# A two-layer encoder on one core: two kinds of 64-row matrix products become 128-row products

## The chip, the cores and the metric

The kernel runs on one core of one Trainium2 chip. The metric is the device time of one execution in microseconds (us), the median over several runs. A TensorE product of a 128-row operand contracts over 128 partitions, that is over all rows of the array; a 64-row product contracts over 64 partitions and uses half the rows. "Rows" of an operand are partitions throughout, and "columns" is the length that streams through the array (256 or 512 here).

## The reference

The program computes two residual layers for x of 1024 steps by 1024 features: layer 0 is a bidirectional Hyena mixer (a gated long convolution by FFT), layer 1 a bidirectional Mamba-2 SSD mixer. The change touches layer 0 alone, in the network that makes the convolution's filters and in the first stage of the transforms:

```python
def hyena_filters(L, w1, b1, w2, b2, w3, b3, freq, w_out):
    ...
    h = jnp.sin(fr * (h @ w3.astype(jnp.float32) + b3))
    h = h @ w_out.astype(jnp.float32)
    ...
    h = h * jnp.exp(-t * jnp.concatenate([deltas, deltas]))
    return h[:, :D_INNER], h[:, D_INNER:]

def bidirectional_fftconv(u, h_fwd, h_bwd, skip):
    ...
    k_f = jnp.fft.rfft(kfull, n=n, axis=0)
    u_f = jnp.fft.rfft(uf32, n=n, axis=1)
    y = jnp.fft.irfft(u_f * k_f[None], n=n, axis=1)[:, :L]
    return y + uf32 * skip.astype(jnp.float32)
```

The hidden layer has 64 features, D_INNER is 2048, L is 1024.

## The kernel before

Matrix products run on float32r operands. Each float32 operand is split into a high part H of 12 significant bits and a low part L, and a product is H.H + H.L + L.H, summed in PSUM. A name that ends in h or l is such a part (`xh`, `xl`, `wh`, `wl`, `tah`, `tal`).

**Two parts on top of each other.** Where only 64 rows are contracted, the parts can share the 128 rows. The filter network's last hidden layer, `hs`, holds H in one half of the partitions and L in the other. A product of `hs` over all 128 rows with the output weights' high part `wfh`, stacked twice, gives H.H + L.H at once. What is missing, H.L, is a second product with the low part `wfl`, over the 64 rows that hold H. In `stage1` these are lines 375 and 376, twice per task, 512 columns each. The first stage of the forward transform does the same in `hyena_fft` from its later calls on: line 589 multiplies the input's stacked parts by `tau`, the table's high part stacked twice, and line 590 the input's high half by `tal`, the table's low part (64 rows, 256 columns), four such pairs per task. Earlier calls, before `tau` is loaded, use three 64-row products (line 592).

**Stages of layer 0.** From about 62 to 317 us the filters are made: for each of 4 blocks of 512 channels, 8 tasks `stage1` (lines 368 to 399: filter products, times a decay `dec` to `kr` on VectorE, split into `xh`, `xl`, three products with `tah`/`tal`, copy to `asb`, to DRAM as `ask`) and 16 tasks `stage2` (load `bs` from `ask`, split, products with `tbh`/`tbl`, copy, to DRAM as `kd`). After that, for 8 blocks of 256 channels: `hyena_mid` (tasks "m", which load `k` from `kd`), `hyena_fft` (tasks "a") and `hyena_back` (tasks "b", whose products with `tai` at lines 642 and 643 have 128 rows and 256 columns), in the order of the list `todo`. The projections of x (line 261, 3072 products of 128 rows and 512 columns) are laid between these tasks by `fill`, a fixed number of quarters per step, so that TensorE has work while a task's other engines run.

**Order.** A scheduler puts the program's instructions into one fixed order per engine when it is built, and each engine then takes its own in that order. Loads and stores are issued by SyncE (SP) in one order; the tables come over GpSimd (POOL). `TB = 12` says before which item of `todo` the table `tau` is fetched; a one-element copy on POOL makes that fetch wait for a product's result (`self.mark`).

**Memory.** `tah` lies in a pool at the right side that is closed when the filters are done. `tal` lies in the pool `h0` that lives as long as layer 0's mixer. The tables and tiles of the later tasks lie in the pool `h1`, opened when the filters are done.

Of the kernel before, what the change touches and what calls it, by code (L numbers as in the profile page):

```python
"""Hybrid encoder trunk, two layers on one core: a bidirectional Hyena layer, then a bidirectional
Mamba-2 SSD layer, each with its DeepNorm residual.

Matrix products run on float32r operands: each float32 operand is split into a high part of 12
significant bits and the rest (x = H + L), and a product is H.H + H.L + L.H in float32 PSUM.

Hyena's long convolution is evaluated at the 1024 points z_g = exp(-2 pi i (g + 1/4) / 1024). With
z^1024 = -i the products of a real signal and a two-sided real kernel wrap into the imaginary part,
so one complex transform of length 1024 gives the linear convolution of length 2048. The transform
is two stages (64 x 16) of matrix products, with t = 16 t1 + t2 and g = g1 + 64 g2.  # L10
"""
# [9 lines left out]
F32 = mybir.dt.float32  # L21
F32R = mybir.dt.float32r
AF = mybir.ActivationFunctionType
ALU = mybir.AluOpType
PSUM = bass.MemoryType.PSUM
DRAM = bass.MemoryType.DRAM

L = 1024
# [6 lines left out]
TA = 3  # L35
# [53 lines left out]
def _round12(a):  # L89
    """float64 -> float32 values with 12 significant bits, nearest even."""  # L90
    m, e = np.frexp(a)
    return np.ldexp(np.rint(m * 4096.0), e - 12).astype(np.float32)
# [40 lines left out]
def _constants():  # L133
# [4 lines left out]
    # both parts side by side, the high one first where n2 is even  # L138
# [34 lines left out]
class Pipe:  # L173
    """Tasks under way, each a generator that yields between its stages; a step moves each by a stage."""
# [15 lines left out]
class Build:  # L190
    def __init__(self, tc, a, p, pp, dp):
        """p, pp, dp: pools in SBUF (weights' tiles), PSUM and DRAM for the whole program."""
        self.tc, self.nc, self.a, self.p, self.pp, self.dp = tc, tc.nc, a, p, pp, dp
        self.ident = p.tile([128, 128], F32, name="ident")
        self.nc.sync.dma_start(out=self.ident, in_=a["ident"])
        self.ready = lambda k: True
        self.mhalf = p.tile([128, 1], F32, name="mhalf")
        self.nc.vector.memset(self.mhalf, -0.5)
# [7 lines left out]
    def weights(self, src, gain=None, pool=None, bufs=2, name="w"):  # L206
        """128 x 1024 (or 512) weights in two parts, times a gain per row if there is one."""
# [14 lines left out]
    def split(self, src, h, l):  # L222
        """h + l = src, both float32r."""
# [3 lines left out]
    def pair(self, pool):  # L227
        """The two parts' tiles of [128, 512] values."""
        return pool.tile([128, 512], F32R, name="xh", bufs=XB), pool.tile([128, 512], F32R, name="xl", bufs=XB)

    def load_pair(self, pool, src):
        """[128, 512] values from DRAM in two parts."""
# [12 lines left out]
    def load_r(self, pool, name, shape, src):  # L245
        """A float32r tile from float32 values that have 12 significant bits."""
# [4 lines left out]
    def projections(self, work, ahead, xh, xl):  # L251
        """Projections of x^T, each [128 channels, 1024] in PSUM for its function; a step per quarter of one."""
# [17 lines left out]
    def filter_mlp(self, pm, hs):  # L270
        """The filter network's last hidden layer at 16 n1 + n2 and at 1024 - (16 n1 + n2), in two parts on top of
        each other."""
# [45 lines left out]
    def filters(self, kd, sh, t):  # L318
        """The convolution kernels' transforms, to kd[block][re/im][64][16][256]; yields the tasks of each step."""
# [3 lines left out]
        def stage2(cb, j):  # L323
            # the last of the first stage's results go to DRAM two steps after their task's first
# [17 lines left out]
        with tc.tile_pool(name="k0", bufs=1) as p:  # L342
# [5 lines left out]
            with tc.tile_pool(name="k1", bufs=1) as p:  # L348

                def consts(cb):  # L350
                    cs = slice(512 * cb, 512 * cb + 512)
                    wfh = [p.tile([128, 512], F32R, name=f"wfh{q}", bufs=2) for q in range(2)]
                    wfl = p.tile([128, 512], F32R, name="wfl", bufs=2)
                    for q in range(2):
# [4 lines left out]
                        nc.scalar.copy(wfh[q], wr)  # L359
                        r = slice(64 * q, 64 * q + 64)  # L360
                        nc.vector.tensor_tensor(out=wfl[r], in0=wr[r], in1=wfh[q][r].bitcast(F32), op=ALU.subtract)
# [6 lines left out]
                def stage1(cb, m, k):  # L368
                    """The kernels at n2 = 2 m and 2 m + 1, and their transforms' first stage."""
                    wfh, wfl, delta, skip = k  # L370
                    ks = [p.tile([128, 512], F32, name=f"kr{i}", bufs=KRB) for i in range(2)]
                    for q in range(2):
                        ps = self.bank()
                        r, c = slice(64 * q, 64 * q + 64), slice(128 * m, 128 * m + 128)
                        nc.tensor.matmul(ps, hs[:, q, c], wfh[q], start=True, stop=False)
                        nc.tensor.matmul(ps, hs[r, q, c], wfl[r], start=False, stop=True)  # L376
# [35 lines left out]
    def hyena(self, yt, after):  # L412
        """Layer 0's mixer up to its output projection: from x^T (permuted time) to y^T in DRAM."""
# [4 lines left out]
        with tc.tile_pool(name="h0", bufs=1) as p, tc.tile_pool(name="hf", bufs=1, space=PSUM) as self.pf:  # L418
# [17 lines left out]
            for n, s in (("ta", [128, 16, 128]), ("tb", [128, 128]), ("tbi", [128, 128])):  # L436
                for q in "hl":
                    t[n + q] = (pa if n + q == "tah" else p).tile(s, F32R, name=n + q)
                    flat = t[n + q].rearrange("p a b -> p (a b)") if len(s) == 3 else t[n + q]
                    if n == "ta":  # L440
                        # not before x
# [5 lines left out]
            def u_work(b):  # L447
                """x1 * v for 256 channels."""
# [9 lines left out]
            def q_work(b):  # L458
                """x0 * silu(z) for 256 channels."""
# [14 lines left out]
            def fill(n):  # L474
                """Projections up to n quarters in all."""
# [23 lines left out]
            with tc.tile_pool(name="h1", bufs=1) as pf:  # L499
                tabs = [(i, n, pf.tile(s, F32R, name=n), d) for i, n, s, d in (  # L500
                    (TA, "tai", [128, 16, 128], "tai"), (TB, "tau", [128, 16, 128], "tauh"))]
# [17 lines left out]
                for i, item in enumerate(todo):  # L519
                    if tabs and i == tabs[0][0]:  # L520
                        # a table's load waits for the products under way
# [41 lines left out]
    def hyena_fft(self, sh, t, us, spill, pb2):  # L563
        """A quarter of the first stage of the transform of 256 channels, to DRAM."""
# [7 lines left out]
        both = "tau" in t  # L572
# [11 lines left out]
        for i in range(2):  # L584
            for hf in range(2):
                n2 = 4 * pb2 + 2 * i + hf
                r = slice(64 * hf, 64 * hf + 64)
                if both:
                    nc.tensor.matmul(pa[hf][:, i], t["tau"][:, n2], u[hf][:, i], start=True, stop=False)
                    nc.tensor.matmul(pa[hf][:, i], t["tal"][r, n2], u[hf][r, i], start=False, stop=True)  # L590
# [8 lines left out]
    def hyena_mid(self, sh, p, t, kd, b, spill, vspill, j):  # L599
        """The transform's second stage, its product with the filters', and the inverse's first, to DRAM."""  # L600
# [29 lines left out]
    def hyena_back(self, sh, p, t, yt, b, vspill, qs, gs, pb2):  # L630
        """A quarter of the inverse's second stage times qs, to yt in the order of time."""
# [44 lines left out]
    def ssd(self, h1t, wdt, yt, after):  # L676
        """Layer 1's mixer up to its output projection: from h1^T to the normed y^T in DRAM; the first steps of what
        comes after are taken beside its last chunks."""
        tc, nc, a = self.tc, self.nc, self.a
        with tc.tile_pool(name="s", bufs=1) as p, tc.tile_pool(name="sf", bufs=1, space=PSUM) as self.pf:  # L680
# [10 lines left out]
            # the exponents' factors: in each direction, rows of ones (2), of the columns' terms (16)  # L691
            # against rows of the sums (2), and of the heads' places (16); odd chunks in the lower half
# [9 lines left out]
            # whether y^T's rows k, k + 1 are in DRAM for the first blocks  # L702
# [6 lines left out]
            # B, C, B^T and x at each chunk  # L709
# [19 lines left out]
            def flow():  # L729
# [7 lines left out]
                def column(ps, w, k, halves):  # L737
                    """What one k adds to 128 channels."""
# [5 lines left out]
                # the first two go through the first half of the time, then through the second  # L744
# [33 lines left out]
            def fill(n):  # L778
                """The order's units up to n quarters in all."""
# [18 lines left out]
            with tc.tile_pool(name="sc", bufs=1) as self.ps:  # L798
# [9 lines left out]
                def places(g):  # L808
                    """The group's rows of the exponents' factors."""
# [13 lines left out]
                for n in range(4):  # L823
# [4 lines left out]
                    else:  # L828
                        # the projections' input has been read
# [26 lines left out]
    def ssd_dt(self, p, h1t, t, wdt):  # L856
        """dt, the chunks' running sums of dt * a in both directions, and what follows of them."""
# [6 lines left out]
        # the second half of the time lies below the first: 64 heads x 512 steps each  # L864
# [32 lines left out]
        def columns(src):  # L897
            """[128, 2, 4, 64]: the heads along each row of the chunks."""
# [48 lines left out]
        def spread(c):  # L947
            """The chunk's exp(running sums) to DRAM, its heads of a parity together."""
# [395 lines left out]
```

## Time before, and how to read the profile

| | |
|---|---|
| time, median of 3 runs | 2263.41 us (2261.83 to 2263.8) |
| profiled execution, first to last instruction (span) | 2258.7 us |
| median less the span | 4.7 us |
| TensorE (PE) busy in the span | 2161.1 us (96%) |
| weight loads (PEld), beside the products | 1676.8 us (74%) |
| VectorE (DVE) | 1596.6 us (71%) |
| ScalarE (ACT) | 1172.2 us (52%) |
| GpSimd (POOL) | 333.5 us (15%) |
| mean granted TensorE clock | 0.981 |

The profiled execution has no time of its own in the records beside its span; what lies around the span is taken as the 4.7 us by which the median is longer.

In the views, `L376` is line 376 of the kernel, `64*128 64x512` is a product whose stationary operand has 64 rows and 128 columns and whose moving operand has 64 rows and 512 columns. A product's record starts when its turn in the array's queue comes, and its modelled end overlaps the next one's start, since products are pipelined. So what a product costs its engine is read from one start to the next, not from the duration. PEclk is the granted clock: 1.00 is the higher of the two levels, 2.4 GHz, 0.50 the lower, 1.2 GHz.

### The profile page before, as it was taken

The page shows a single profiled execution, that of the slowest core. Times are in us where ns is not written, and L with a number is a line of the kernel's source. Part 1 is how long each engine was busy: PE and PEld are TensorE (multiplying, and loading weights), DVE is VectorE, ACT ScalarE, POOL GpSimd, SP SyncE. Part 2 cuts the span into 40 slices and gives each one's busy share as a digit, 9 for nine tenths or more (in the row PEclk, how much of TensorE's full clock was granted, in tenths as well). Part 3 has the DMA queues.
Part 4 walks back from the last instruction along what each step waited for, and adds up shares of the span by engine and source line. Part 5 has one row for each costly group of instructions (what it writes and reads, how often), then busy time and mean ns, then how long its engine had stood idle before and what let it go on. Part 6 is the DMA issues. An engine that isn't in the chain of part 4 may idle for free.

```text
span 2258.7 us, 28866 instructions
## 1 busy us (share of the span) xinstructions
PE 2161.1 (96%) x9930; PEld 1676.8 (74%) x9930; DVE 1596.6 (71%) x2269; ACT 1172.2 (52%) x1688; POOL 333.5 (15%) x390
## 2 busy tenths in 40 slices
PE   8999999999999999999999997999999998887897
PEld 5677677878787878778777776777777776565686
DVE  7888877676766768657866564764876877765665
ACT  4677775455655555446654343645455555333442
POOL 0000000000000000000000102333344445534000
PEclk9999999999999999999999998999999999888999
DMA  6266778565656556557686425434455455446863
GB/s 201 100 216 229 238 250 258 174 195 159 188 156 177 167 161 177 149 167 207 232 303 202 147 64 156 124 110 127 142 153 163 154 150 166 147 156 197 265 218 128
DMA packets 261423, 399.26 MB, mean 177 GB/s; under 512 B 31879, under 2 KB 158599, under 8 KB 260765
## 3 DMA queue, kind: packets, MB, share of 16 engines
q1 hardware_dynamic: 247677, 391.38, 55.6%
q0 software_dynamic: 13600, 6.04, 1.2%
q8 instruction: 79, 1.29, 0.2%
q14 instruction: 67, 0.55, 0.1%
HBM read 280.64 MB, written 116.65 MB: 176 GB/s over the span
## 4 chain that ended last, share of the span: by engine, by line
PE 80%; DMA 9%; DVE 6%; ACT 2%; issue 2%; POOL 1%; SPq 0%; POOLq 0%; DVEq 0%; ACTq 0%
PE pj L261 31%; PE pj L743 16%; PE pj L1193 5%; PE pk L1193 5%; PE f L241 3%; PE f L242 3%; PE f L243 3%; DMA wr<-l_w_out 3%; DMA bx<-bxd 2%; PE f L1024 2%; PE f L1085 1%; PE f L996 1%; PE f L590 1%; PE f L1059 1%; PE f L376 1%
## 5 line engine op out<-in xcount | busy, mean ns | idle before, releaser
L261 PE MATMUL pj<-xth,wh 128*128 128x512 f32 x1024 | 329.3, 400 | 1.8 <-ACT xth L224 1.8
L261 PE MATMUL pj<-xtl,wh 128*128 128x512 f32 x1024 | 328.5, 398 | 1.4 <-DVE xtl L225 1.4
L261 PE MATMUL pj<-xth,wl 128*128 128x512 f32 x1024 | 325.6, 395 | 0.0
L215 DVE TENSOR_TENSOR wl<-wr,wh 128x1024 fp32r<-128x1024 f32 x152 | 192.1, 1266 | 153.0 <-ACT wh L214 151.3
L214 ACT CAST wh<-wr 128x1024 fp32r<-128x1024 f32 x152 | 159.5, 1049 | 190.0 <-PE pj L261 60.7
L261 PEld LDWEIGHTS pj<-xtl,wh 128*128 128x128 f32 x1024 | 192.3, 189 | 48.7 <-issue 4.6
L261 PEld LDWEIGHTS pj<-xth,wl 128*128 128x128 f32 x1024 | 192.2, 188 | 46.7 <-issue 4.6
L261 PEld LDWEIGHTS pj<-xth,wh 128*128 128x128 f32 x1024 | 188.6, 189 | 45.1 <-issue 3.8
L743 PE MATMUL pj<-h1th,wh 128*128 128x512 f32 x640 | 217.3, 413 | 0.9 <-DVE cv L671 0.9
L743 PE MATMUL pj<-h1th,wl 128*128 128x512 f32 x640 | 207.0, 400 | 0.0
L743 PE MATMUL pj<-h1tl,wh 128*128 128x512 f32 x640 | 206.9, 401 | 0.0
L225 DVE TENSOR_TENSOR xl<-bs,xh 128x512 fp32r<-128x512 f32 x192 | 129.2, 686 | 60.3 <-ACT xh L224 59.2
L1241 POOL TENSOR_SCALAR rs<-mv 128x1 f32<-128x1 f32 x16 | 8.3, 518 | 1019.8 <-DMA wr<-l_w_out 740.3
L224 ACT CAST xh<-bs 128x512 fp32r<-128x512 f32 x192 | 117.5, 620 | 67.5 <-PE f L642 29.0
L743 PEld LDWEIGHTS pj<-h1th,wh 128*128 128x128 f32 x640 | 118.8, 192 | 40.5 <-issue 18.6
L743 PEld LDWEIGHTS pj<-h1tl,wh 128*128 128x128 f32 x640 | 122.2, 192 | 28.4 <-issue 2.7
L743 PEld LDWEIGHTS pj<-h1th,wl 128*128 128x128 f32 x640 | 122.5, 193 | 27.2 <-issue 1.4
L559 DVE SCALAR_TENSOR_TENSOR cv<-pj,cw,cv 128x960 f32<-128x960 f32 x192 | 139.2, 744 | 4.8 <-ACT cv L556 2.7
L671 DVE SCALAR_TENSOR_TENSOR cv<-pj,cw,cv 128x1023 f32<-128x1023 f32 (+1 forms) x96 | 122.5, 1276 | 6.2 <-ACT cv L668 5.7
L1193 PE MATMUL pj<-wh,yh 128*128 128x512 f32 x320 | 105.5, 411 | 16.9 <-ACT wh L217 9.3
L1193 PE MATMUL pj<-wl,yh 128*128 128x512 f32 x320 | 104.5, 406 | 2.5 <-DVE wl L218 2.0
L1193 PE MATMUL pj<-wh,yl 128*128 128x512 f32 x320 | 102.8, 403 | 0.0
(264 smaller groups left out, 4226.2 us busy)
## 6 DMA issues: line engine op xcount, KB each, us to landing
wr<-w SPq DMA_DIRECT2D x104, 512.0 KB
wr<-l_w_out SPq DMA_DIRECT2D x96, 512.0 KB
k<-kd SPq DMA_DIRECT2D x256, 128.0 KB
ask<-asb SPq DMA_DIRECT2D x64, 256.0 KB
bs<-ask SPq DMA_DIRECT2D x64, 256.0 KB
kd<-asb SPq DMA_DIRECT2D x64, 256.0 KB
as<-asb SPq DMA_DIRECT2D x64, 256.0 KB
bs<-as SPq DMA_DIRECT2D x64, 256.0 KB
```

What stands on the lines that cost most here:

```text
L214: nc.scalar.copy(wh, wr)
L215: nc.vector.tensor_tensor(out=wl, in0=wr, in1=wh.bitcast(F32), op=ALU.subtract)
L224: self.nc.scalar.copy(h, src)
L225: self.nc.vector.tensor_tensor(out=l, in0=src, in1=h.bitcast(F32), op=ALU.subtract)
L241: mm(out, ah, bh, start=start, stop=False)
L242: mm(out, ah, bl, start=False, stop=False)
L243: mm(out, al, bh, start=False, stop=stop)
L261: self.nc.tensor.matmul(ps[:, t], lhs[:, k], rhs[:, k, t], start=st, stop=sp)
L559: nc.vector.scalar_tensor_tensor(out=acc[:, o], in0=ps[:, i], scalar=cw[:, w:w + 1], in1=acc[:, o], op0=ALU.mult, op1=ALU.add)
L671: nc.vector.scalar_tensor_tensor(out=acc[:, o], in0=ps[:, i], scalar=cw[:, w:w + 1], in1=acc[:, o], op0=ALU.mult, op1=ALU.add)
L743: nc.tensor.matmul(ps[:, c], lhs[:, k], rhs[:, k, c], start=st, stop=sp)
L1193: nc.tensor.matmul(po[hf], lhs[:, t], rhs[:, c], start=s, stop=e)
```

## The change

The low parts get the same form as the high ones. `wfl` becomes two tiles of 128 rows (the output weights' low part stacked twice, one tile for each of the two halves q), and line 376 multiplies all 128 rows of `hs` with it. The transform's low table is loaded stacked twice as well (`taul`, a new 1 MB load; the array that it comes from is there before), and line 590 multiplies all 128 rows. The sum then holds L.L besides. `tal`, which only the filters and the earlier calls of `hyena_fft` now use, moves to the pool that is closed with `tah`.

```diff
-                    wfl = p.tile([128, 512], F32R, name="wfl", bufs=2)
+                    wfl = [p.tile([128, 512], F32R, name=f"wfl{q}", bufs=2) for q in range(2)]
...
-                        nc.scalar.copy(wfh[q], wr)
-                        r = slice(64 * q, 64 * q + 64)
-                        nc.vector.tensor_tensor(out=wfl[r], in0=wr[r], in1=wfh[q][r].bitcast(F32), op=ALU.subtract)
+                        self.split(wr, wfh[q], wfl[q])
...
-                        r, c = slice(64 * q, 64 * q + 64), slice(128 * m, 128 * m + 128)
+                        c = slice(128 * m, 128 * m + 128)
...
                         nc.tensor.matmul(ps, hs[:, q, c], wfh[q], start=True, stop=False)
-                        nc.tensor.matmul(ps, hs[r, q, c], wfl[r], start=False, stop=True)
+                        nc.tensor.matmul(ps, hs[:, q, c], wfl[q], start=False, stop=True)
...
-                    t[n + q] = (pa if n + q == "tah" else p).tile(s, F32R, name=n + q)
+                    t[n + q] = (pa if n == "ta" else p).tile(s, F32R, name=n + q)
...
-                    (TA, "tai", [128, 16, 128], "tai"), (TB, "tau", [128, 16, 128], "tauh"))]
+                    (TA, "tai", [128, 16, 128], "tai"), (TB, "tauh", [128, 16, 128], "tauh"), (TB, "taul", [128, 16, 128], "taul"))]
...
-                    if tabs and i == tabs[0][0]:
+                    while tabs and i == tabs[0][0]:
...
-        both = "tau" in t
+        both = "taul" in t
...
-                    nc.tensor.matmul(pa[hf][:, i], t["tau"][:, n2], u[hf][:, i], start=True, stop=False)
-                    nc.tensor.matmul(pa[hf][:, i], t["tal"][r, n2], u[hf][r, i], start=False, stop=True)
+                    nc.tensor.matmul(pa[hf][:, i], t["tauh"][:, n2], u[hf][:, i], start=True, stop=False)
+                    nc.tensor.matmul(pa[hf][:, i], t["taul"][:, n2], u[hf][:, i], start=False, stop=True)
```

Apart from names and a shift of lines by one, the engines' orders are the same in both programs but for three places. The first is none of order but of operands: TensorE's first filter products, at the start of the stage from 62 us on. Before:

```order
L375 MATMUL f<-wfh_292,hs 128x512
L376 MATMUL f<-wfl,hs 128x512
L375 MATMUL f<-wfh_291,hs 128x512
L376 MATMUL f<-wfl,hs 128x512 x2
L375 MATMUL f<-wfh_292,hs 128x512
L376 MATMUL f<-wfl,hs 128x512
```

With the change:

```order
L374 MATMUL f<-wfh_292,hs 128x512
L375 MATMUL f<-wfl_293,hs 128x512
L374 MATMUL f<-wfh_291,hs 128x512
L375 MATMUL f<-wfl_294,hs 128x512
L375 MATMUL f<-wfl_293,hs 128x512
L374 MATMUL f<-wfh_292,hs 128x512
L375 MATMUL f<-wfl_294,hs 128x512
```

The products stand as they stood; the two that read one tile `wfl` before (its two halves) read a tile each now. (The shape printed is the output's, so it does not tell the rows.)

The second place is POOL's fetch of the tables, from `tai` on. Before:

```order
L523 CAST tai<-asb 1x2
L524 DMA tai<-tai 128x2048
L523 CAST tau<-asb 1x2
L524 DMA tau<-tauh 128x2048
```

With the change:

```order
L522 CAST tai<-asb 1x2
L523 DMA tai<-tai 128x2048
L522 CAST tauh<-asb 1x2
L522 CAST taul<-asb 1x2
L523 DMA tauh<-tauh 128x2048
L523 DMA taul<-taul 128x2048
```

The second table's one-element copy and its load stand beside the first's.

The third place is SP's queue at the end of the filters, where the first load of `k` for `hyena_mid` stands among the last block's stores (`ask`, `kd`) and loads (`bs`). Before, with what each row waits for:

```order
L340 DMA kd<-asb 128x2x256 [waits DMAHW1_49,DVE_49]
L397 DMA ask<-asb 128x512 [waits DMAHW2_49,Activation_49]
L340 DMA kd<-asb 128x2x256 [waits DMAHW3_49,Activation_49]
L609 DMA k_3480<-kd 64x512 [waits DMAHW4_49]
L340 DMA kd<-asb 128x2x256 [waits DMAHW5_49,DVE_49]
L234 DMA bs<-ask 128x512 [waits DMAHW6_49,DMAHW2_49,DMAHW0_49]
```

With the change:

```order
L340 DMA kd<-asb 128x2x256 [waits DMAHW0_49,DVE_49]
L396 DMA ask<-asb 128x512 [waits DMAHW1_49,Activation_49]
L340 DMA kd<-asb 128x2x256 [waits DMAHW2_49,Activation_49]
L608 DMA k_3485<-kd 64x512 [waits DMASW5_49,DMASW4_49,DMAHW3_49,PE_49,Pool_49]
L608 DMA k_3485<-kd 64x512 [waits DMAHW4_49]
L340 DMA kd<-asb 128x2x256 [waits DMAHW5_49,DVE_49]
L234 DMA bs<-ask 128x512 [waits DMAHW7_49,DMAHW6_49,DMAHW1_49]
```

The first half of the first `k` stood five stores earlier before; now both halves stand behind the last store of `ask`, and the tile's memory is that in which `tah` and `tal` lay (it waits for their loads, for TensorE and for POOL). Some dozens of rows of the engines around this place stand a few positions earlier or later for it. Beyond that only one split of weights at the start of layer 1 changes places with two others.

## Rows read from the trace of the kernel before

**Rows 1.** The page's head: the span and the number of instructions.

```profile
span 2258.7 us, 28866 instructions
```

**Rows 2.** Busy time by stretch; columns: engines' busy us (instructions), PEclk, DMA share.

```profile
60.00:310.00 250.00, 249.93 (x1016) 175.37 (x1015) 216.76 (x318) 183.35 (x310) 0.00 (x0) 1.00 0.61 202
310.00:490.00 180.00, 178.24 (x796) 144.52 (x796) 134.54 (x196) 100.87 (x156) 1.41 (x4) 1.00 0.72 221
490.00:1005.00 515.00, 514.84 (x2332) 409.79 (x2331) 348.78 (x501) 275.87 (x426) 0.00 (x0) 1.00 0.57 167
...
2000.00:2100.00 100.00, 74.27 (x305) 54.78 (x304) 54.08 (x77) 31.41 (x44) 33.89 (x34) 0.86 0.65 196
```

**Rows 3.** TensorE's waits, whole span: us in total, times, longest.

```profile
PE f L241 <- ACT xh L224: 1.8, 4, 0.8
```

**Rows 4.** Timeline of TensorE at 211 us: start, duration, instruction, count.

```profile
210.64 0.39 PE L243 MATMUL f<-xh,tbl 128*128 128x512 f32 x1
...
211.58 0.40 PE L375 MATMUL f<-wfh,hs 128*128 128x512 f32 x1
211.90 0.50 PE L376 MATMUL f<-wfl,hs 64*128 64x512 f32 x1
212.33 0.50 PE L261 MATMUL pj<-xtl,wh 128*128 128x512 f32 x1
212.67 0.63 PE L261 MATMUL pj<-xth,wl 128*128 128x512 f32 x2
```

**Rows 5.** Line 376 alone: durations min/median/max in ns, first and last start.

```profile
L376 PE MATMUL f<-wfl,hs x64: 490/496/502, 63.5 to 306.2; 64*128 64x512 f32 x64
```

**Rows 6.** Timeline of TensorE at 804 us, one task of `hyena_fft`.

```profile
803.72 0.28 PE L589 MATMUL f<-xh,tau 128*128 128x256 f32 x1
803.93 0.38 PE L590 MATMUL f<-xh,tal 64*128 64x256 f32 x1
...
806.12 0.50 PE L261 MATMUL pj<-xth,wh 128*128 128x512 f32 x1
806.45 0.60 PE L570 MATMUL f<-ident,cv 128*128 128x128 f32 x4
```

**Rows 7.** Timeline of TensorE at 422 us, one task of `hyena_back`.

```profile
421.70 0.28 PE L642 MATMUL f<-xh,tai 128*128 128x256 f32 x1
421.82 0.28 PE L643 MATMUL f<-xl,tai 128*128 128x256 f32 x1
...
422.66 0.62 PE L261 MATMUL pj<-xth,wh 128*128 128x512 f32 x2
```

**Rows 8.** Line 590 alone, columns as in rows 5.

```profile
L590 PE MATMUL f<-xh,tal x48: 379/382/385, 491.4 to 1000.5; 64*128 64x256 f32 x48
...
L590 PE MATMUL f<-xl,tal x48: 378/381/383, 492.0 to 1001.2; 64*128 64x256 f32 x48
```

**Rows 9.** VectorE's groups, 60 to 310 us: busy, mean ns, idle before and releasers.

```profile
L381 DVE TENSOR_TENSOR kr<-f,dec 64x512 f32<-64x512 f32 x127 | 87.2, 687 | 3.7 <-ACT dec L378 1.0 <-PE f L376 0.2
L225 DVE TENSOR_TENSOR xl<-kr,xh 128x512 fp32r<-128x512 f32 x62 | 41.9, 687 | 17.2 <-ACT xh L224 17.1
...
L361 DVE TENSOR_TENSOR wfl<-bs,wfh 64x512 fp32r<-64x512 f32 x8 | 5.5, 686 | 0.9 <-ACT wfh L359 0.7
```

**Rows 10.** POOL's timeline at the table's load.

```profile
410.16 0.53 POOL L524 DMA_DIRECT2D tau<-tauh  x1 [0.30 <-POOL tau L523]
```

**Rows 11.** DMA issues: KB each, median us to landing.

```profile
tau<-tauh POOLq DMA_DIRECT2D x1, 1024.0 KB, 7.2
```

**Rows 12.** SP's timeline at the filters' end.

```profile
321.13 0.48 SPq L609 DMA_DIRECT2D k<-kd  x1
```

**Rows 13.** The chain that ended last, there: start, us, what.

```profile
322.35 4.42 DMA bs<-ask
```

**Rows 14.** The tile `tai` alone, weight loads, columns as in rows 5.

```profile
L642 PEld LDWEIGHTS f<-xh,tai x128: 186/190/193, 421.5 to 1114.6; 128*128 128x128 f32 x128
```

**Rows 15.** Timeline of TensorE at 64 us, the first filter products.

```profile
64.32 0.50 PE L376 MATMUL f<-wfl,hs 64*128 64x512 f32 x2
```

## The prediction, on record before the run

> **What bounds the kernel now.** I read the busy time by stretch first, because the page's 96% for TensorE is a mean over stages. The change touches products between 62 and 306 us (line 376) and between 491 and 1001 us (line 590) [rows 5, 8]. In the stretch from 60 to 310 us TensorE is busy for 249.93 of 250 us, and from 490 to 1005 us for 514.84 of 515 us, at PEclk 1.00 in both [rows 2]. TensorE's waits say the same: the longest kind that falls in the filters and transforms is a wait for a cast, 1.8 us in four pieces [rows 3]. So TensorE sets the time there, and whatever shortens its queue shortens the kernel, until another engine fills up. VectorE is the candidate: 216.76 of 250 us in the filters, but only 348.78 of 515 us (68%) in the later stage [rows 2].
>
> Busy does not mean fast, so next I read the timeline from start to start around a 64-row product. Four products of 128 rows and 512 columns run from 210.64 to 211.58 us, 0.235 us each. Then the start of the 64-row product at 211.90 comes 0.32 us after that of the 128-row product before it, the next 128-row product starts 0.43 us after that, and the one behind it another 0.34 us later [rows 4]. Three products take 1.09 us instead of 0.705. The 64-row product does half the work and costs 0.385 us on top of its own slot, spread over itself and both neighbours. Records of a product overlap where the array is kept full; here they hardly do. The array seems to run empty when the number of rows changes, in both directions, and the weights for the next form seem to be loaded only then.
>
> In the transform the same shows at 256 columns. Eight products that alternate between 128 and 64 rows start at 803.72 us, the next product starts at 806.12, and the one behind it at 806.45 [rows 6]: 2.40 us, and then 0.33 where 0.235 is usual. Eight products of 128 rows and 256 columns, in the inverse transform, take 421.70 to 422.66 us, 0.96 us [rows 7].
>
> **The change, part by part.** *Filter products:* 64 of them [rows 5], in the same places of TensorE's order. If a 128-row `wfl` product runs like any other, each saves 0.385 us: 64 x 0.385 = 24.6 us.
>
> *Transform products:* 96 [rows 8], in tasks of four. A task saves 2.40 + 0.10 - 0.96 = 1.54 us; 24 tasks make 37.0 us. Together 61.6 us of TensorE's queue.
>
> A rule of the Trainium skill speaks against this sum. "TensorE: Matmul & The Clock Gate", section "Why this matters for your kernels", says that a product over 32 rows takes as long as one over 128, and that few rows pay only when several such products run at once in different row groups. By that the two forms would cost the same, the saving would be 0, and the one place where two 64-row products do run at once would be lost. The trace differs: 1.09 us against 0.705 for three products.
>
> That one place is at 64.32 us: two products by `wfl` share a record of 0.50 us, so one of them was free [rows 15]. With 128 rows it needs a slot, 0.235 us. The 61.6 us contain such irregular groups (runs without line 261 between them), so I leave it in the rounding.
>
> *VectorE.* The split of the output weights runs on 128 instead of 64 rows, 8 times. It is paid by columns: 64x512 takes 686 ns, and 128x512 at line 225 takes 687 [rows 9]. Cost nothing. What counts is that its work stays while the stage shrinks: 216.8 us in 249.9 - 24.6 = 225.3 us, 96%. The lower bound of what this costs is 0, since 216.8 is less than 225.3. For the upper bound VectorE keeps all the idle time that it now spends on the casts of `kr` by ScalarE, 17.1 us [rows 9]: 216.8 + 17.1 = 233.9, so 8.6 us come back. Those casts stand in ScalarE's queue behind copies of TensorE's results, which come earlier when TensorE is faster, and a task's transform products stand some three steps behind its filter products; that gives slack. But the margin is thin, so I take 4 us, near the middle. What is late then is `xh`, `xl` of the filters at lines 241 to 243, and the projections behind them.
>
> In the transform stage VectorE has 348.8 us of work in 515 - 37 = 478 us, 73%; I take nothing there.
>
> *The second table.* 1 MB over POOL's queue, behind the first. The first was issued at 410.16 us and landed 7.2 us later [rows 10, 11]; the second is issued some 0.53 us after that and, if it only follows the first, is there by about 426 us. It is first read at 491.4 us [rows 8], about 25 us earlier in the new time, but so is the load: some 65 us of cover remain. POOL had nothing else to do from 60 to 310 us and 1.41 us from 310 to 490 [rows 2]. Cost nothing; without that cover it would be one wait of about 7 us.
>
> *The queue at the filters' end.* Both halves of the first `k` now stand behind the last `ask`, one of them moved there from five stores earlier. The wait for `tah` and `tal` is no new one: the store ahead of it already needs the last product that reads them. But the last block's loads `bs` come one issue later, 0.48 us [rows 12], and the chain runs through such a load: 4.42 us from 322.35 us [rows 13], before one of the waits of [rows 3]. I take 0.5 us; bounds 0 and 2 (four such waits).
>
> *Sum.* -24.6 - 37.0 + 4 + 0.5 = -57.1 us. The profiled execution's span is 2258.7 us [rows 1], so 2201.6 us after; with the 4.7 us by which the median lies above it, 2263.4 - 57.1 = 2206 us. Layer 1 starts earlier by the same amount and is unchanged.
>
> **The rivals.** *VectorE takes over the filters, and the clock falls.* From 2000 to 2100 us, where TensorE stands still for 25.7 us in many pieces, PEclk is 0.86 on average [rows 2]; in the filters it is 1.00 now. With VectorE's upper bound TensorE would stand still for 8.6 of 233.9 us there. Without a fall that is 2211 us; with 0.86 throughout, TensorE alone would need 225.3 / 0.86 = 262.0 us, 36.7 more than in the sum without losses: 2263.4 - 61.6 + 36.7 + 0.5 = 2239 us. Against it: from 310 to 490 us TensorE also waits, 1.8 us in all, and PEclk stays 1.00 [rows 2]; and in the filters the projections lie between the waits.
>
> *Weight loads bound the 256-column products.* A load's record is 190 ns [rows 14], a slot 120. If loads of changing weights could not overlap, a task would take 8 x 0.19 = 1.52 us and save 0.98 instead of 1.54: 13 us less, 2219 us. Against it: in [rows 7] the weights change at every second product (642 and 643 share a slice of `tai`, the next pair takes another), and the slots are all 0.12 us.
>
> *The rows are not the cause.* Then the change does nothing: the switch of tables, or a port, makes the gaps, and the time is 2263.4 + 0.5 = 2264 us. For it: the 128-row products next to it are slow as well. Against it: [rows 7] and the first products of [rows 4] change tables without a gap. The rule of the Trainium skill that stands above would end here, too.
>
> *Slower.* The place is the filters, the mechanism the clock. The gain is gone when TensorE's time there, 225.3 us at 1.00, grows by 61.6 us, that is from a mean clock of 225.3 / 286.9 = 0.79 down; at 0.75 it grows by 75 us, net 13.5 us and 2277 us. No stretch of [rows 2] has a mean so low, and the lowest of them lies where TensorE stands still for a quarter of the time.
>
> **How the numbers follow.** The forecast, 2202 to 2211 us (VectorE's bounds), 0.78. A larger gain, 2196 to 2202, from the last stage, whose clock falls and rises in any case: 0.04. VectorE with the clock, 2211 to 2239: 0.07. Weight loads, 2219: 0.04. No effect, 2264: 0.05. Slower, 2277: 0.02. From 2199 to 2216 us lie the forecast and about half of each of its two neighbours (the clock's case is likelier near its lower end), 0.83. A measurement of this kernel tells about 0.2% (4.5 us) from no change: faster 0.93, same 0.05, slower 0.02.
>
> **What would show it.** Right: line 375's and 376's products start 0.23 to 0.24 us apart, those of 589 and 590 0.12 us; a task of eight takes about 0.96 us; the last product by `wfl` starts near 286 instead of 306 us (306.2 - 24.6 + 4); the transform's last product by the low table comes near 944 instead of 1001 us; PEclk stays 1.00 in layer 0. VectorE's share from 60 to 290 us near 95%, TensorE's waits there about 4 us in all, on casts or splits. Wrong: gaps remain at 128 rows (another cause); TensorE waits for `xl` or `kr` for more than 9 us; line 590 waits for `taul`; PEclk below 1.00 before 1000 us.

## The result, and the profile after

The changed kernel takes 2206.24 us (median of 4 runs, 2204.04 to 2212.62) against 2262.95 us of the kernel before beside it on the same chip (4 runs, 2261.83 to 2263.8). The ratio is 0.9755, with a 95% interval of 0.9738 to 0.9772: 56.7 us less. The forecast was 2206.

The head of the page of the changed kernel: span and instructions, then busy time, share of the span and instructions of each engine.

```profile
span 2204.7 us, 28875 instructions
...
PE 2102.7 (95%) x9930; PEld 1668.1 (76%) x9930; DVE 1594.9 (72%) x2269; ACT 1169.8 (53%) x1688; POOL 331.5 (15%) x392
```

TensorE has as many products as before, 9930, and 58.4 us less busy time; the weight loads' fell by 8.7 us, no other engine's moved by more than 2.5. So the gain is in how long the same number of products takes.

The timeline of TensorE in the changed kernel, at a place that answers to [rows 4] (columns: start, duration, instruction, count):

```profile
197.27 0.40 PE L243 MATMUL f<-xh,tal 128*128 128x512 f32 x1
197.51 0.39 PE L374 MATMUL f<-wfh,hs 128*128 128x512 f32 x1
197.74 0.39 PE L375 MATMUL f<-wfl,hs 128*128 128x512 f32 x1
197.96 0.40 PE L261 MATMUL pj<-xtl,wh 128*128 128x512 f32 x1
198.20 0.40 PE L261 MATMUL pj<-xth,wl 128*128 128x512 f32 x1
```

Read it from start to start: 0.24, 0.23, 0.22, 0.24 us. The 0.32, 0.43 and 0.34 us of [rows 4] are gone, from the product itself and from both neighbours. A task of `hyena_fft` in the changed kernel, answering to [rows 6]:

```profile
756.28 0.28 PE L588 MATMUL f<-xh,tauh 128*128 128x256 f32 x1
756.40 0.28 PE L589 MATMUL f<-xh,taul 128*128 128x256 f32 x1
...
757.11 0.28 PE L589 MATMUL f<-xl,taul 128*128 128x256 f32 x1
757.23 0.29 PE L569 MATMUL f<-ident,cv 128*128 128x128 f32 x1
```

Eight products take 0.95 us where they took 2.40, like the inverse transform's in [rows 7]. The lines of the low parts alone, answering to [rows 5, 8] (durations min/median/max in ns, first and last start):

```profile
L375 PE MATMUL f<-wfl,hs x64: 387/392/398, 63.5 to 284.1; 128*128 128x512 f32 x64
...
L589 PE MATMUL f<-xh,taul x48: 277/282/287, 468.0 to 943.5; 128*128 128x256 f32 x48
...
L589 PE MATMUL f<-xl,taul x48: 279/283/285, 468.2 to 943.8; 128*128 128x256 f32 x48
```

The last filter product starts 22.1 us earlier (306.2 before), the last of the transform's 57.4 us earlier (1001.2 before). The weight loads (PEld) show the lost time from another side. Waits of PEld in the kernel before, 60 to 310 us (total us, times, longest):

```profile
PEld f L376 <- issue: 20.5, 63, 0.4
PEld pj L261 <- issue: 11.1, 46, 0.2
```

"issue" means that the profile shows nothing that the engine waited for, no data and no semaphore. Such a wait stands ahead of 63 of the 64 products of 64 rows, and 46 times at the projection that follows one. The changed kernel's list for the same stretch has neither row; its longest are these:

```profile
PEld f L241 <- ACT xh L224: 3.5, 12, 0.6
PEld f L241 <- issue: 2.6, 7, 0.4
PEld f L374 <- ACT asb L395: 2.2, 12, 0.2
PEld f L241 <- ACT asb L395: 2.0, 3, 0.8
```

Busy time by stretch, answering to [rows 2] (columns as there: PE, PEld, DVE, ACT, POOL, then PEclk, DMA share, GB/s):

```profile
60.00:290.00 230.00, 229.16 (x1027) 178.95 (x1026) 215.91 (x320) 185.52 (x311) 0.00 (x0) 1.00 0.66 221
...
460.00:950.00 490.00, 489.15 (x2375) 407.00 (x2375) 355.59 (x510) 278.07 (x435) 0.00 (x0) 1.00 0.59 178
60.00:310.00 250.00, 249.03 (x1110) 194.40 (x1109) 229.75 (x340) 198.48 (x332) 0.00 (x0) 1.00 0.67 224
```

PEclk stays 1.00 up to 1082 us; the one fall in layer 0 comes then, in its output projection (see below). VectorE works 215.91 of 230 us in the filters, 94%; the forecast said near 95%. Yet TensorE stands still for only 0.84 us there. To see where the time came from, I counted TensorE's products from the start of each trace and took the start of the same number in both (us, profiled executions):

| product | before | after | difference |
|---|---|---|---|
| 1200th, end of the filters | 309.5 | 287.1 | -22.4 |
| 2000th, ahead of the first `taul` product | 490.7 | 467.4 | -23.3 |
| 4400th, behind the last one | 1021.7 | 964.0 | -57.6 |
| 5000th, layer 0's output projection | 1155.2 | 1100.4 | -54.7 |
| end of the span | 2258.7 | 2204.7 | -54.0 |

So the filters gave 22 to 23 us, the transforms 34 (57.6 - 23.3), and 3.6 us were given back behind them in this pair of executions. The medians differ by 56.7 and not by 54.0: the execution profiled before was a short one of its kernel. (The changed kernel's profiled execution took 2206.51 us, 1.8 more than its span; with the same 1.8, an estimate, the one before took 2260.5.)

### The profile page after: what moved, and what is told of

It is laid out like the page before. It is cut to its first block, busy times and chain, and to the rows that moved or that the text cites. A ratio compares the mean times of both kernels' runs of the same rounds, so it can differ in the third digit from the quotient of the medians.

```text
span 2204.7 us, 28875 instructions
## 1 busy us (share of the span) xinstructions
PE 2102.7 (95%) x9930; PEld 1668.1 (76%) x9930; DVE 1594.9 (72%) x2269; ACT 1169.8 (53%) x1688; POOL 331.5 (15%) x392
## 4 chain that ended last, share of the span: by engine, by line
PE 80%; DMA 9%; DVE 6%; ACT 2%; issue 2%; POOL 1%; SPq 0%; POOLq 0%; DVEq 0%; ACTq 0%
PE pj L261 30%; PE pj L742 17%; PE pj L1192 6%; PE pk L1192 5%; PE f L241 3%; PE f L243 3%; PE f L242 3%; DMA wr<-l_w_out 3%; DMA bx<-bxd 2%; PE f L1023 2%; PE f L995 2%; PE f L1084 2%; PE f L1058 1%; DVE wl L215 1%; DMA bxd<-tr 1%
```

## The experiments

Each was run beside the kernel before on the same chip: 2263.41 us (2260.76 to 2266.14) for the first four, 2262.72 (2259.51 to 2265.47) for the next three, 2262.05 (2260.37 to 2267.21) for the last. **The theory** is that TensorE pays when the number of rows in use changes, about 0.385 us for a run of 64-row products, in and out together. **The rivals**: each 64-row product costs that much by itself; or the loss is only that the half array left free isn't used at the same time.

**Each half of the change alone.** The first takes the filter products, the second the transform's (cut to the product that changes):

```diff
 # filters only
...
-                        nc.tensor.matmul(ps, hs[r, q, c], wfl[r], start=False, stop=True)
+                        nc.tensor.matmul(ps, hs[:, q, c], wfl[q], start=False, stop=True)
 # transform only
...
-                    nc.tensor.matmul(pa[hf][:, i], t["tal"][r, n2], u[hf][r, i], start=False, stop=True)
+                    nc.tensor.matmul(pa[hf][:, i], t["taul"][:, n2], u[hf][:, i], start=False, stop=True)
```

> The kernel before with the filter products alone at 128 rows; the transform keeps its 64-row products. By the theory of the prediction (a 128-row product has no gap around it): 64 x 0.385 = 24.6 us less, of which the trace with the whole change shows 22 us arriving, so about 2240 us and a last filter product near 284 us; the transform's tasks of eight still take about 2.4 us. By the rival that the two edits need each other, or that the gain is all in the transform: near 2263 us.

> The kernel before with the transform's low table alone at 128 rows, with its second 1 MB load; the filters keep their 64-row products. By the theory: 96 x 0.385 = 37 us less at most, and the trace with the whole change shows 34 us gained there, so 2226 to 2229 us. If the second table or the moved loads of k cost anything by themselves, the time is above 2229 us by it, and line 590's first product waits. This run and the one with the filters alone should add up to the whole change's 57 us if VectorE's share in the filters does not couple them.

Measured: 2240.22 us for the filters (2239.57 to 2240.64; ratio 0.9895, 0.9881 to 0.991), 23.2 less; 2227.83 for the transform (2227.17 to 2231.61; 0.984, 0.9824 to 0.9856), 35.6 less. The sum is 58.8, the whole change gave 56.7: within the intervals they add up. So neither part hides behind the other, and the second table's load costs nothing visible.

**Both 64-row products of a pair behind each other.** Nothing about a product changes; only the order does, so that the rows change half as often.

```diff
         for i in range(2):
+            if both:
+                for hf in range(2):
+                    nc.tensor.matmul(pa[hf][:, i], t["tau"][:, 4 * pb2 + 2 * i + hf], u[hf][:, i], start=True, stop=False)
             for hf in range(2):
...
                 if both:
-                    nc.tensor.matmul(pa[hf][:, i], t["tau"][:, n2], u[hf][:, i], start=True, stop=False)
                     nc.tensor.matmul(pa[hf][:, i], t["tal"][r, n2], u[hf][r, i], start=False, stop=True)
```

> The kernel before with the same products of 64 rows in the transform, in another order: two by the high table, then two by the low one, twice per task, so 2 runs of 64-row products per task instead of 4. If the cost belongs to the change of the number of rows (0.385 us for each run of 64-row products, in and out): 24 tasks x 2 x 0.385 = 18.5 us less, 2244 us; if besides the two of a run, which use different halves of the rows, run at the same time, another 24 x 2 x 0.12 = 5.8 us, 2239 us. If the cost belongs to each 64-row product itself: no change, 2263 us. If only running at the same time counts, as a rule of the Trainium skill has it (TensorE: Matmul & The Clock Gate, section Why this matters for your kernels): 5.8 us, 2257 us.

Measured: 2242.62 us (2240.5 to 2243.75; ratio 0.9905, 0.989 to 0.992), 20.8 less, without one 64-row product fewer. The timeline of TensorE in this kernel:

```profile
513.27 0.28 PE L587 MATMUL f<-xh,tau 128*128 128x256 f32 x1
513.39 0.28 PE L587 MATMUL f<-xl,tau 128*128 128x256 f32 x1
513.60 0.38 PE L592 MATMUL f<-xh,tal 64*128 64x256 f32 x1
513.60 0.38 PE L592 MATMUL f<-xl,tal 64*128 64x256 f32 x1
513.91 0.39 PE L587 MATMUL f<-xh,tau 128*128 128x256 f32 x1
514.13 0.28 PE L587 MATMUL f<-xl,tau 128*128 128x256 f32 x1
```

Two things show. The two 64-row products, in different halves of the rows, start together and cost one slot. And the time is lost at the two borders: 0.21 us into the run where 0.12 is usual, 0.31 out of it, and 0.22 for the next start. Both rivals fail: a price per product would have given nothing, and the shared slot alone is 48 x 0.12 = 5.8 us. The price belongs to the run. Runs and shared slots together were expected to give 24.3 us. The trace shows why it is less: 22 of the 24 tasks have the new order, and in the two others, whose eight products the scheduler split by other work, the rows still change at every product. 22 tasks of 24 make 22.3 us, which lies within the interval of the ratio (some 3.4 us to either side of 20.8).

**All of the transform with 64 rows.** Every call of `hyena_fft` takes the form of the early ones, twelve 64-row products and no stacked table, so that a task has one border in and one out. (The split of a task's input then takes two operations on ScalarE and VectorE instead of four.)

```diff
-            tables.close()
...
-                    (TA, "tai", [128, 16, 128], "tai"), (TB, "tau", [128, 16, 128], "tauh"))]
+                    (TA, "tai", [128, 16, 128], "tai"),)]
...
+                            tables.close()
```

(The last line stands behind the last `hyena_fft`, so that `tah` stays until then.)

> The kernel before with three 64-row products everywhere in the transform, as its first eight tasks have them: 12 products of 64 rows in one run per task, none of 128, the tables of the filters kept instead of the stacked one (and the split of the input over 128 rows on ScalarE and VectorE, two operations instead of four). If the cost belongs to the change of the number of rows: 12 x 0.12 + 0.385 = 1.83 us per task instead of 2.50, 24 x 0.67 = 16 us less, 2247 us, although three times as many products have 64 rows. If it belongs to each 64-row product: 12 x (0.12 + 0.385) = 6.06 us per task, 24 x 3.56 = 85 us more, 2348 us.

Measured: 2231.36 us (2229.04 to 2232.57; ratio 0.9855, 0.9841 to 0.987), 32 less, where I had expected 16. The timeline of TensorE in this kernel shows a later task, and below it an early one:

```profile
510.76 0.39 PE L241 MATMUL f<-xh,tah 64*128 64x256 f32 x2
510.99 0.28 PE L242 MATMUL f<-xl,tah 64*128 64x256 f32 x2
...
511.45 0.28 PE L243 MATMUL f<-xh,tal 64*128 64x256 f32 x2
511.67 0.51 PE L261 MATMUL pj<-xth,wh 128*128 128x512 f32 x1
...
157.06 0.39 PE L243 MATMUL f<-xh,tal 128*128 128x512 f32 x1
157.38 0.38 PE L241 MATMUL f<-xh,tah 64*128 64x256 f32 x1
157.60 0.28 PE L242 MATMUL f<-xl,tah 64*128 64x256 f32 x1
157.72 0.27 PE L243 MATMUL f<-xh,tal 64*128 64x256 f32 x1
...
158.86 0.28 PE L243 MATMUL f<-xh,tal 64*128 64x256 f32 x1
159.07 0.50 PE L241 MATMUL f<-xh,tbh 128*128 128x512 f32 x1
159.41 0.40 PE L242 MATMUL f<-xl,tbh 128*128 128x512 f32 x1
```

My sizing had taken the early form: one half of the rows after the other, 157.38 to 159.41 us, 2.03 us to the second product behind. Here the scheduler put products of the two halves by turns ("x2" are two products that start within one record), and twelve of them take 0.91 us, 510.76 to 511.67. The borders are there all the same. Twelve 64-row products in that order take hardly longer than eight of 128 rows (0.95 us), and the second table isn't needed for it. From the 2000th product to the one that answers to the 4400th this trace takes 499.3 us, the kernel before 531.0, the changed one 496.6.

**Filters with 128 rows, transform with 64.** The changed kernel with the three edits above: if the borders are the whole matter, it should equal the change.

> The filter products at 128 rows as in the change, but the transform with twelve 64-row products in one run per task, as in the run that had 64 rows everywhere. In that run the two halves of the rows ran beside each other, 3 to 13 ns apart, and a task took as long as one at 128 rows (1.07 to 1.26 us up to the second product behind it, against 1.06 to 1.19). If the gains add up: 2231 - 23 = 2208 us, within 5 us of the change, without its second table. If the change's 128 rows in the transform are worth something by themselves beyond the missing gaps: above 2213 us.

Measured: 2210.97 us (2205.07 to 2214.08; ratio 0.977, 0.9754 to 0.9787). On the same chip the changed kernel itself ran once more:

> The changed kernel once more, on the chip of the next two runs, so that they have it beside them: 2206 us, last filter product near 284 us.

Measured: 2207.85 us (2203.71 to 2210.62; ratio 0.9763, 0.9749 to 0.9776). The intervals overlap, so the times don't tell the two apart. The traces do, by little: the stretch from the 2000th product to the one that answers to the 4400th takes 499.1 us here and 499.3 in the all-64 form, against 496.6 and 496.8 in the changed kernel's two traces. Of the 34.3 us that the change gains there, some 32 come from the rows no longer changing product by product; the 128 rows themselves, which also do away with the last border of each task, add 2 to 3.

**VectorE relieved.** The forecast took 4 us for VectorE. Of the copies of the second stage's results half are made by ScalarE, half by VectorE (`EV = 'av'`, line 333 takes them by turns); here all go to ScalarE.

```diff
-EV = 'av'
+EV = 'a'
```

> The changed kernel with all of the filters' second-stage copies on ScalarE (half were on VectorE, 21 of 690 ns in the stretch, 14.5 us). If VectorE's load is what cost the filters 2 to 3 us of the 24.6: that comes back, last filter product near 282 us, 2204 us. If the loss is made of TensorE's short stops for ScalarE's casts and copies: none of it comes back and the longer queue of ScalarE costs some more, last filter product at 284 us or later, 2206 to 2212 us.

Measured: 2207.64 us (2204.73 to 2209.71; ratio 0.9758, 0.9745 to 0.9771), as with the change. Its window from 60 to 310 us, and its longest wait of TensorE there:

```profile
60.00:310.00 250.00, 245.00 (x1090) 186.42 (x1090) 213.98 (x314) 207.80 (x357) 0.00 (x0) 1.00 0.69 227
```

```profile
PE f L241 <- ACT xh L224: 3.8, 5, 1.7
```

VectorE has 16 us less to do, ScalarE 9 more, and the 1200th product starts at 289.8 us instead of 286.9 (the changed kernel beside it). In the filters of this trace it lost 3 us: TensorE's waits there, all for ScalarE, are 4.7 us instead of 0.8. It tells nothing against a limit of VectorE, only that there is nothing to be had by this way.

**VectorE loaded.** The other direction, with `EV = 'v'`: all those copies on VectorE, 32 more of 0.69 us each (the mean of its own copies of this kind in the changed kernel), 22 us.

> The changed kernel with all of the filters' second-stage copies on VectorE, the other way round from the run with all of them on ScalarE. VectorE then has some 15 us more in the filters' 225 us, 97% or more. If VectorE's load is what holds the filters back: TensorE's 1200th product, at 287 us with the change, comes at 290 to 300 us, time 2210 to 2220 us. If it is ScalarE's queue of casts and copies: the 1200th product at 286 us or earlier, 2204 to 2206 us.

Measured: 2223.29 us (2221.86 to 2225.12; ratio 0.9822, 0.9804 to 0.9839), some 15 us more than the change by the two ratios, and 3 above the expected range. Its windows, and its longest wait of TensorE in the first:

```profile
60.00:310.00 250.00, 237.74 (x1028) 182.29 (x1027) 235.20 (x354) 178.00 (x297) 0.00 (x0) 0.98 0.63 211
...
150.00:210.00 60.00, 51.87 (x211) 37.33 (x212) 55.94 (x87) 42.01 (x74) 0.00 (x0) 0.95 0.74 242
```

```profile
PE f L241 <- DVE kr L380: 4.9, 7, 1.2
```

The 1200th product starts at 307.9 us: 20.8 us later than with the change, where I had expected 3 to 13. (The expectation counted only the 21 copies of the stretch, 15 us; up to the 1200th product VectorE has 22 us more to do.) TensorE does 1028 products here in these 250 us, hardly more than the 1016 of the kernel before [rows 2], with VectorE at work for 94% of the stretch. And the first rival of the prediction is seen at work: from 150 to 210 us TensorE stands still for 8 us in pieces and the granted clock is 0.95 on average. From 60 to 310 us TensorE stands still for 12.3 us; 6.6 us of its waits there end with VectorE, 5.5 with ScalarE. At the mean clock of 0.98 another 5 us are lost (an estimate: 0.02 of 250). So VectorE's limit is real and close. Its busy share does not show it: in the changed kernel it is 94% too, from 60 to 290 us, and TensorE hardly waits.

Not tried: the eight early tasks with 128 rows, for which the stacked tables would have to lie in SBUF beside the filters' tiles; the same tasks with the two halves by turns; and a 128-row form of layer 1's products of 18 rows (below).

## Why the prediction was right

**The cost of a 64-row product, 0.385 us on top of its slot: right**, and so was reading it off the neighbours. Summed over the trace before, the 64 filter products and their two neighbours take 24.6 us beyond their usual slots, 0.384 each (with 0.232 us as the slot, the usual time from start to start). The paired order and the all-64 form show that it is a price of the change of rows, and the weight loads' waits for "issue" show the same from the other side: 31.6 us of them in the filters before, in 109 pieces, none of these rows after. The prediction's other rivals fail in the rows shown: in the changed kernel the table changes at every product of a task, `tauh` and `taul` by turns, and the starts are 0.12 us apart, so neither the switch of tables nor weight loads of 0.19 us made the gaps.

The page "TensorEngine Tiling (Array Packing)" of the Trainium skill, section "Key Properties", says that a change of the tiling mode drains the engine. The traces agree, with 0.385 us per run. The rule that the prediction held against itself, in "TensorE: Matmul & The Clock Gate", "Why this matters for your kernels", holds too, but inside a run: a 64-row product of 256 columns takes 0.12 us like one of 128 rows (157.60 to 157.72 us in the all-64 form), and two in different halves of the rows start together. By it alone the change would have given 0, since it says nothing about the border.

**Filters, -24.6 with +4 for VectorE, so -20.6:** measured -22.4 at their end. The place that the forecast named for the loss was wrong. It looked for 4 us of TensorE waiting for casts and splits; TensorE stands still for 0.84 us there, and its one wait in the list is 0.7 us for a copy. The missing 2.2 us lie in TensorE's starts: beyond their slots the 64 products and their neighbours still take 0.9 of the 24.6 us, and the other products of the stage take 6.1 us where they took 4.9. Two stops, at 156.4 and 236.3 us, are 0.4 and 0.5 us of this; both end with a copy by ScalarE (line 395), the 0.7 us of the list. The rest are pieces of 0.13 us and less. ScalarE in turn waits longer for VectorE's `kr` than before (13.5 us from 60 to 310 us, against 5.8), so how much of the 2.2 goes back to VectorE stays open.

**The transform, -37.0:** mis-sized by about 3, measured -34.3 between the 2000th and the 4400th product. Summed over the 24 tasks, the time that the eight products and the two behind them take beyond their usual slots (0.232, 0.119 and 0.109 us for 512, 256 and 128 columns) fell from 36.6 to 1.3 us, so 35.3 of the 37.0 are found in the tasks themselves. The forecast gave each task 0.10 us for the product behind; where a transpose of 128 columns stands there, it is 0.055. Most of the 1.3 us is one stop of 0.9 behind a task, for a copy by ScalarE (line 626). The 1.0 between 35.3 and 34.3 is spread over the stage's other products, at most 0.08 us at one.

**The order at the filters' end, +0.5: not there.** From the 1200th to the 2000th product the changed kernel gained 0.9 us more. SP's timeline in the changed kernel, answering to [rows 12]:

```profile
298.49 1.09 SPq L608 DMA_DIRECT2D k<-kd  x2
299.68 0.53 SPq L340 DMA_DIRECT2D kd<-asb  x1
300.32 0.40 SPq L234 DMA_DIRECT2D bs<-ask  x1
```

Both halves of `k` stand ahead of the store and the load, as foreseen, and take 1.09 us to issue, of which one half's 0.48 stood there before. TensorE's list of waits from 285 to 335 us has one row, where the stretch before had the 1.8 us of [rows 3]:

```profile
PE f L241 <- ACT xh L224: 0.5, 1, 0.5
```

The later load shows up in no wait.

**The second table, 0: right.** Its issue on POOL's timeline, and its landing in the list of DMA issues (KB, median us):

```profile
386.95 0.54 POOL L523 DMA_DIRECT2D taul<-taul  x1
```

```profile
taul<-taul POOLq DMA_DIRECT2D x1, 1024.0 KB, 9.5
```

It is there by 396.5 us and first read at 468.0: 71 us of cover, where 65 were worked out.

**The split of the output weights over 128 rows, 0: right.** VectorE's group in the changed kernel, to be held against the 686 ns of [rows 9]:

```profile
L225 DVE TENSOR_TENSOR wfl<-bs,wfh 128x512 fp32r<-128x512 f32 x8 | 5.2, 686 | 0.7 <-ACT wfh L224 0.7
```

**Layer 1, unchanged: nearly.** The trace shown gives back 3.6 us between the 4400th product and the end, 2.9 of it before the 5000th, still in layer 0. There, from 1079.5 us on, TensorE stands still for 1.49 us, waiting for a cast of the output projection's weights (line 214), and the granted clock falls behind it:

```profile
1082.00:1086.00 4.00, 3.94 (x11) 2.99 (x11) 3.70 (x5) 3.31 (x5) 0.00 (x0) 0.61 0.92 332
```

At that place the products start 0.427 us apart instead of 0.23, which costs 1.6 us; the longer wait costs 1.3. In the kernel before, the stop there is shorter and the clock stays 1.00, with 18 products in the same four us (1138 to 1142). So "PEclk stays 1.00 in layer 0" came out up to 1082 us only. In the profile of the repeated run the clock stays 1.00 there, and the gain is 56.9 us at the 4400th product (964.8 us) and 56.8 at the end (span 2201.9 us): nothing given back. Why the weights come later in one execution than in another stays open.

So the forecast was right in the mechanism and in both large terms; of the small ones, the -37.0 was 2.7 us too large, and the filters with their transition gave 3.2 us more than the forecast's -20.1 (-24.6 + 4 + 0.5; measured -23.3 at the 2000th product). That the sum of -57.1 fell within 0.4 us of the measured -56.7 is these two nearly cancelling, and luck: the trace shown gives back 3.6 us behind the change, the repeated one nothing.

## What to carry to other kernels

Look at the products on both sides of one that uses fewer rows: what it costs stands in their starts, not in its own record. Where small products of fewer rows lie singly among products of all rows, either fill the rows (stack the operand, here with its low part, at no cost on the engines that prepare it) or put the small ones together, the two halves by turns; here the second needed no further table and gave 32.0 us where the first gave 35.6 in the transform. And before counting such a gain, ask which engine is next: here VectorE was at 94% of the filters' time, and 22 us more of work for it took 15 us of the gain back.

## What the runs showed of the hardware beyond that

Two 64-row products in different halves of the rows ran in one slot only where they followed each other directly: in the all-64 form twelve took 0.91 us by turns, and 1.69 us one half after the other (157.38 to 159.07 us). An early task in which four pairs met took 1.15 us (at 265.5 us).

The same border stands in layer 1, untouched by the change. The timeline of TensorE in the changed kernel, at a pair of products of 18 rows:

```profile
1589.96 0.59 PE L995 MATMUL f<-xw,bx 128*128 128x512 f32 x1
1590.48 0.50 PE L1058 MATMUL f<-er,eb 18*128 18x512 f32 x2
1590.92 0.73 PE L742 MATMUL pj<-h1th,wh 128*128 128x512 f32 x2
1591.48 0.39 PE L742 MATMUL pj<-h1tl,wh 128*128 128x512 f32 x1
```

The two start within one record, and the next product of 128 rows starts 0.44 us after them; the slot of 0.235 us is exceeded at 18 rows as at 64. There are 128 such products.
